# Four elementwise products and sums moved from GpSimd to VectorE in a hybrid retention and gated DeltaNet layer

## The chip, the cores and the metric

The kernel runs on one core of a Trainium2 chip. The metric is the device time of one execution in microseconds (us). Five engines of the core work side by side, each on its own list of instructions: TensorE (PE, with its weight loads shown as PEld), VectorE (DVE), ScalarE (ACT), GpSimd (POOL) and SyncE (SP), which here issues most transfers. The profile records one execution, with the clock that was granted to TensorE (1.00 is 2.4 GHz, 0.50 is 1.2 GHz).

## The reference

One decoder layer for a sequence of T = 1024 positions and a model width of 2048, all in fp32:

```python
h = x * (1 + scale) + shift                      # adaLN from c
[ret_q|ret_k|ret_v|ret_g|gdn_qkv|gdn_g|gdn_a|gdn_b] = h @ W_in
# 4 retention heads (q, k 128 wide, v 256 wide)
q, k = rotary(q), rotary(k)                      # t1*cos - t2*sin, t1*sin + t2*cos
o_ret = GroupNorm(chunkwise_retention(q, k, v)) * silu(ret_g)
# 8 gated DeltaNet heads of width 128
q, k, v = silu(causal_conv4(gdn_qkv)); q, k = l2norm(q), l2norm(k)
o_gdn = RMSNorm(chunked_delta_rule(q, k, v, decay, beta)) * silu(gdn_g)
y = concat(o_ret, o_gdn) @ W_out
out = LayerNorm(alpha * x + gate * y)
```

## The kernel before, in words

Every large matmul is done in three: an fp32 operand is split into a high part (hi) and a rest (lo), and hi·hi, hi·lo and lo·hi are summed. The weights come in units. `w_unit` loads a unit of fp32 weights by SP (`w_raw`), ACT casts it to `w_hi` (L94), and DVE subtracts to get `w_lo` (L95); each of the two has two buffers. So PE needs ACT and DVE once for every unit of weights.

The stages, in order of time: the conditioning sums, loading and transposing of x and the first projections (0 to about 197 us); `gemm_v` for the values of retention head 0 (L508, to about 245 us); eight DeltaNet heads, each with four projections `gemm_cm` (L476) and about 109 us long (to about 1107 us), with the work of retention head 0 woven into the first of them; retention heads 1 to 3 (to about 1562 us); the output projection (L1120, to about 1914 us), whose operands are split by ACT (L1065) and DVE (L1067); and a tail of DVE work.

The smaller steps are Python generators (rotary and retention, `gdn_keys`, `gdn_merge`, `gdn_scan`, `gdn_out`) that are advanced by `tick()` between the matmuls of the projections. PE's order is thus written out by hand (`tc.manual_schedule(engines={PE})`); the order on the other engines is chosen by a scheduler when the kernel is built, in which L94, L95 and the weight loads have high priority.

The names that matter here:
- `rotary` (L545 to L554) makes two products per half of the sequence into `thr` (L550, L551), one into `yr` (L552) and adds them (L553). Its table `rot` shares a buffer with the values `vt`, which ACT starts to fill at L1006.
- `retention_out` (L642 to L658): PE transposes into PSUM, ACT scales into `mxr` (L654), L656 multiplies with the gate `sg`, and a DMA issued from POOL's queue stores it (L435). `mxr` has one buffer for heads 0 to 2, so L654 of one block waits until the store of the block before has landed. The second gate tile shares its buffer with the DeltaNet values `vs` (L909), which therefore wait for its last reader at L656.
- `gdn_keys` and `gdn_merge` solve a triangular system: PE makes `sup` with DVE (L814), DVE solves blocks of 32 (`X`, L834 to L840), SP sends the result through DRAM to `Pm` (L843, L846), DVE transposes it (`Tm`, L858), and PE merges the blocks (L868).
- `gdn_scan` (L914 to L973) makes `et` (L924), transposes the queries (L929), scales them in place by a row of decays (L932), and then runs the state from chunk to chunk (PE L945, L951, L957; DVE L947, L962).
- `gdn_out` (L977 to L995): a reciprocal root `f` (L117 to L119), the product `og*f` (L985), transposes on PE (L991), the gate on DVE (L993), and a store (L435).

The lines around the four that the diff touches:

```python
S.copy(hi[:, :n], raw[:, :n])                                   # L94, ACT
V.tensor_tensor(out=lo[:, :n], in0=raw[:, :n], in1=hi[:, :n].bitcast(F32), op=ALU.subtract)   # L95
tag, bufs = ("gb", 2) if r == RH - 1 else ("mx", 1)              # retention_out
```

Of the kernel before, what the change touches and what calls it, by code (L numbers as in the profile page):

```python
# [11 lines left out]
ALU = mybir.AluOpType  # L12
# [46 lines left out]
def hybrid_layer_kernel(ctx: ExitStack, tc: tile.TileContext, x, c, w_ada, b_ada, w_in, gdn_conv_w,  # L59
# [3 lines left out]
    V, S, G, PE = nc.vector, nc.scalar, nc.gpsimd, nc.tensor  # L63
# [370 lines left out]
    def store(out, in_):  # L434
        nc.gpsimd.dma_start(out=out, in_=in_)  # L435

    def small_ps():
        return ps.tile([P, 512], F32, name="ps", tag="ps")
# [106 lines left out]
    def rotary(pt, rot, tag="th", bufs=2):  # L545
        y = mp.tile([P, T], F32, name="yr", tag="y", bufs=3)
        for i in range(2):
            sl = slice(i * 512, (i + 1) * 512)
            th = mp.tile([P, 512], F32, name="thr", tag=tag, bufs=bufs)
            V.tensor_tensor(out=th[0:64], in0=pt[64:128, sl], in1=rot[0:64, 1, sl], op=ALU.mult)  # L550
            V.tensor_tensor(out=th[64:128], in0=pt[0:64, sl], in1=rot[64:128, 1, sl], op=ALU.mult)  # L551
            V.tensor_tensor(out=y[:, sl], in0=pt[:, sl], in1=rot[:, 0, sl], op=ALU.mult)  # L552
            G.tensor_tensor(out=y[:, sl], in0=y[:, sl], in1=th, op=ALU.add)  # L553
        return y  # L554

    def retention(r, q, k, vt, sgs):
# [85 lines left out]
    def retention_out(r, pr, os_, sgs, es):  # L642
        po2 = small_ps()
        n = len(os_) * 256
        for i, e in enumerate(es):
            for j in range(2 * len(os_)):
                c0 = i * n + j * P
                PE.transpose(po2[:, c0:c0 + P], os_[j // 2][:, j % 2, e * P:(e + 1) * P], ident)
        tsl = slice(2 * pr * P, 2 * pr * P + n)
        for i, e in enumerate(es):  # L650
            kti = 2 * r + e
            tag, bufs = ("gb", 2) if r == RH - 1 else ("mx", 1)
            mx = mp.tile([P, n], F32, name="mxr", tag=tag, bufs=bufs)
            S.activation(out=mx, in_=po2[:, i * n:(i + 1) * n], func=AF.Identity,  # L654
                         scale=gnp[:, kti:kti + 1], bias=gnp[:, 8 + kti:9 + kti])
            G.tensor_tensor(out=mx, in0=mx, in1=sgs[e][:, tsl], op=ALU.mult)  # L656
            store(out=mixed[kti][:, tsl], in_=mx)
            yield 0  # L658

# [72 lines left out]
    B4 = [P, 4, P]  # L732

    def c4(t):
        return t.rearrange("p (c i) -> p c i", i=P)
# [178 lines left out]
    def gdn_scan(h, st, k, q, dec, Pm):  # L914
        kt_, vs, co = st["kt"], st["vs"], st["co"]
        *rows, et = gates.pop(h)
        ssq = gp.tile([P, NC], F32, name="ssq", tag="ssq")
        for hf in range(2):
            c4s = slice(4 * hf, 4 * hf + 4)
            pqk = small_ps()  # L920
            for j in range(4):
                cl = slice((4 * hf + j) * P, (4 * hf + j + 1) * P)
                PE.matmul(pqk[:, j * P:(j + 1) * P], k[:, cl], q[:, cl], start=True, stop=True)  # L923
            V.tensor_tensor(out=et[:, c4s], in0=c4(pqk), in1=et[:, c4s], op=ALU.mult)  # L924
            yield 2
            pq = small_ps()
            for j in range(4):
                ch = 4 * hf + j
                PE.transpose(pq[:, j * P:(j + 1) * P], q[:, ch * P:(ch + 1) * P], ident)  # L929
            sum_squares(pq, ssq[:, c4s])  # L930
            hs = slice(hf * 512, (hf + 1) * 512)
            G.tensor_tensor(out=q[:, hs], in0=q[:, hs], in1=rows[hf], op=ALU.mult)  # L932
            yield 2 + 6 * hf
        state = None
        for hf in range(2):
            o = mp.tile(B4, F32, name="og", tag="o", bufs=2)
            so = gp.tile([P, 4], F32, name="so", tag="so", bufs=2)
            for j in range(4):
                ch = 4 * hf + j
                cl = slice(ch * P, (ch + 1) * P)  # L940
                if state is None:
                    w = vs[:, ch]
                else:
                    pks = small_ps()
                    PE.matmul(pks[:, :P], k[:, cl], state, start=True, stop=True)  # L945
                    w = gp.tile([P, P], F32, name="w", tag="w", bufs=2)
                    V.scalar_tensor_tensor(out=w, in0=pks[:, :P], scalar=dec["neg"][:, ch, h:h + 1], in1=vs[:, ch],  # L947
                                           op0=ALU.mult, op1=ALU.add)
                    yield HOP[0]
                pu = small_ps()  # L950
                PE.matmul(pu[:, :P], Pm[:, ch], w, start=True, stop=True)  # L951
                u = gp.tile([P, P], F32, name="u", tag="u", bufs=2)
                S.activation(out=u, in_=pu[:, :P], func=AF.Copy, scale=co[:, ch:ch + 1])
                yield HOP[1]
                if ch < NC - 1:
                    pd = small_ps()
                    PE.matmul(pd[:, :P], kt_[:, ch], u, start=True, stop=True)  # L957
                    ns = mp.tile([P, P], F32, name="gs", tag="state", bufs=2)
                    if state is None:
                        V.tensor_copy(ns, pd[:, :P])  # L960
                    else:
                        V.scalar_tensor_tensor(out=ns, in0=state, scalar=dec["egl"][:, ch, h:h + 1], in1=pd[:, :P],  # L962
                                               op0=ALU.mult, op1=ALU.add)
                po = small_ps()
                if state is not None:
                    PE.matmul(po[:, :P], q[:, cl], state, start=True, stop=False)  # L966
                PE.matmul(po[:, :P], et[:, ch], u, start=(state is None), stop=True)  # L967
                state = ns
                S.copy(o[:, j], po[:, :P])
                junk = gp.tile([P, P], F32, name="junk", tag="xt")  # L970
                S.activation(out=junk, in_=po[:, :P], func=AF.Square, accum_out=so[:, j:j + 1])
                yield HOP[2]
            spawn_aux(gdn_out(h, hf, o, so, ssq, st), 1)  # L973

    HOP = (4, 4, 4)

    def gdn_out(h, hf, o, so, ssq, st):  # L977
        hs = slice(hf * 512, (hf + 1) * 512)
        c4s = slice(4 * hf, 4 * hf + 4)
        f = gp.tile([P, 4], F32, name="f", tag="f")  # L980
# [1 line left out]
        V.tensor_scalar(out=xo, in0=ssq[:, c4s], scalar1=1e-6, scalar2=1.28e-4, op0=ALU.add, op1=ALU.mult)  # L982
        V.scalar_tensor_tensor(out=xo, in0=so, scalar=1.0 / P, in1=xo, op0=ALU.mult, op1=ALU.add)
        rsqrt(gp, f, xo, 4, "o")
        G.tensor_tensor(out=o, in0=o, in1=f[:, :, None].broadcast_to(B4), op=ALU.mult)  # L985
        yield 36
        while "sg" not in st:
            yield 1
# [3 lines left out]
        mx = mp.tile([P, 512], F32, name="mxg", tag="mx")  # L992
# [9 lines left out]
    q = rotary(part_q0, rot, "gb", 2)  # L1002
# [15 lines left out]
    for h in range(GH):  # L1018
# [6 lines left out]
        q = conv_silu(gemm_cm(GQ + h * P), h)  # L1025
# [3 lines left out]
    for r in range(1, RH):  # L1029
# [7 lines left out]
        q = rotary(gemm_cm(RQ + r * P, True), rot)  # L1037
        k = rotary(gemm_cm(RK + r * P, True), rot)
        sgs = []
# [56 lines left out]
    for hf in range(2):  # L1096
# [4 lines left out]
        for cb in range(4):  # L1101
# [91 lines left out]
            if not last:  # L1193
                rows = []
                for n, kx in enumerate(korder):
# [15 lines left out]
                    if late and hf == 1:  # L1211
                        f, sl = late.pop(0)
# [52 lines left out]
```

## Time and profile before

| | |
|---|---|
| three runs | 1919.08, 1922.44 and 1927.89 us, median 1922.44 |
| profiled execution | 1927.46 us, its span 1925.7 us |
| mean granted clock of TensorE | 0.99 |
| PE busy | 97% of the span |
| DVE, ACT, POOL busy | 58%, 28%, 6% |

The profile is of one execution, and it is near the longest of the three runs. Matmuls are pipelined, so a row's duration overlaps the next row's; the starts tell the pace. The number in square brackets in a row of a timeline is how long the engine had been idle before it, and what it waited for.

### The profile page before, as it was taken

Reading aid. Unit: us, or ns where it says so; the run is one execution under the profiler, and the core shown is the slowest. Engines: PE = TensorE matmul, PEld = TensorE weight load, DVE = VectorE, ACT = ScalarE, POOL = GpSimd, SP = SyncE. Lnnn points to the kernel's source line nnn. Section 1 sums busy time; section 2 is a strip of 40 time slices with the busy share of each in tenths; the row PEclk is TensorE's granted clock in tenths of the full one; section 3 lists DMA queues with packets and bytes.
Section 4 is the critical chain, followed back from the end, with each engine's and each line's share of the span. In section 5 each row is a group of like instructions: output and inputs, shape, how many; then the busy total and the mean of one; then the engine's idle time right before and its main releaser. Section 6 shows DMA issues by size and latency. Waiting matters only on the chain.

```text
span 1925.7 us, 27778 instructions
## 1 busy us (share of the span) xinstructions
PE 1867.2 (97%) x10336; PEld 1582.6 (82%) x10336; DVE 1109.6 (58%) x2801; ACT 544.5 (28%) x1227; POOL 114.7 (6%) x133
## 2 busy tenths in 40 slices
PE   4999899999999999999999999999999999999997
PEld 3788878888888888888888898898898887888886
DVE  5776666574756657474655643544542544458566
ACT  2543232332323231322322121211211232235321
POOL 0000111000000000000000000100010010000000
PEclk9999999998999999999999999999999999999999
DMA  9994222221222222122212233144141157346622
GB/s 287 324 301 135 74 64 71 46 69 48 64 57 60 50 54 69 45 69 51 64 50 61 53 99 109 45 143 137 39 137 50 34 191 268 105 152 223 215 77 88
DMA packets 242474, 205.87 MB, mean 107 GB/s; under 512 B 44361, under 2 KB 200602, under 8 KB 242082
## 3 DMA queue, kind: packets, MB, share of 16 engines
q1 hardware_dynamic: 239714, 195.70, 34.3%
q0 software_dynamic: 2624, 8.39, 1.2%
q8 instruction: 81, 1.33, 0.3%
q14 instruction: 55, 0.45, 0.1%
HBM read 185.12 MB, written 18.92 MB: 106 GB/s over the span
## 4 chain that ended last, share of the span: by engine, by line
PE 79%; DVE 3%; DMA 1%; issue 0%; ACT 0%; POOL 0%; SPq 0%; POOLq 0%; DVEq 0%; ACTq 0%
PE pg L476 45%; PE po L1120 16%; PE pg L508 7%; DVE yc L666 1%; PE ps L923 1%; PE ps L951 1%; DMA raw<-mixed 1%; PE ps L967 1%; PE ps L957 1%; PE ps L811 1%; PE ps L945 1%; PE ps L966 1%; PE po L1128 1%; PE ps L603 1%; PE ps L896 0%; PE ps L889 0%
## 5 line engine op out<-in xcount | busy, mean ns | idle before, releaser
L476 PE MATMUL pg<-h_hi,w_lo 128*128 128x512 f32 x1376 | 448.0, 400 | 0.0
L476 PE MATMUL pg<-h_hi,w_hi 128*128 128x512 f32 x1376 | 446.9, 399 | 0.0
L476 PE MATMUL pg<-h_lo,w_hi 128*128 128x512 f32 x1376 | 445.0, 400 | 0.0
L1120 PE MATMUL po<-wr,ms 128*128 128x512 f32 x1380 | 314.6, 389 | 1.8 <-ACT wr L1065 1.5
L94 ACT CAST w_hi<-w_raw 128x512 fp32r<-128x512 f32 (+1 forms) x203 | 126.0, 621 | 637.2 <-PE pg L476 493.9
L1120 PEld LDWEIGHTS po<-wr,ms 128*128 128x128 f32 x1380 | 258.8, 188 | 56.3 <-ACT wr L1065 1.9
L476 PEld LDWEIGHTS pg<-h_hi,w_hi 128*128 128x128 f32 x1376 | 255.6, 189 | 49.5 <-ACT w_hi L94 1.7
L476 PEld LDWEIGHTS pg<-h_hi,w_lo 128*128 128x128 f32 x1376 | 255.7, 189 | 48.1 <-issue 0.2
L476 PEld LDWEIGHTS pg<-h_lo,w_hi 128*128 128x128 f32 x1376 | 255.3, 189 | 47.2
L95 DVE TENSOR_TENSOR w_lo<-w_raw,w_hi 128x512 fp32r<-128x512 f32 (+1 forms) x203 | 146.6, 722 | 243.7 <-ACT w_hi L94 198.4
L508 PE MATMUL pg<-w_lo,h_hi 128*128 128x256 f32 (+1 forms) x448 | 128.5, 287 | 3.4 <-DVE w_lo L95 3.4
L1067 DVE TENSOR_TENSOR wr<-raw,wr 128x512 fp32r<-128x512 f32 x116 | 80.6, 702 | 88.7 <-ACT wr L1065 84.5
L508 PE MATMUL pg<-w_hi,h_hi 128*128 128x256 f32 (+1 forms) x448 | 128.9, 288 | 1.4 <-DVE part L324 1.4
L508 PE MATMUL pg<-w_hi,h_lo 128*128 128x256 f32 (+1 forms) x448 | 128.6, 287 | 0.0
L1065 ACT CAST wr<-raw 128x512 fp32r<-128x512 f32 x116 | 71.0, 621 | 130.9 <-PE po L1120 123.2
L666 DVE SCALAR_TENSOR_TENSOR yc<-pg,cw,yc 128x1023 f32<-128x1023 f32 (+2 forms) x69 | 88.3, 1280 | 4.3 <-ACT yc L663 3.0
L508 PEld LDWEIGHTS pg<-w_lo,h_hi 128*128 128x128 f32 x448 | 86.1, 192 | 4.0 <-DVE w_lo L95 3.8
L508 PEld LDWEIGHTS pg<-w_hi,h_hi 128*128 128x128 f32 x448 | 86.1, 192 | 3.7 <-ACT w_hi L94 1.7
L508 PEld LDWEIGHTS pg<-w_hi,h_lo 128*128 128x128 f32 x448 | 86.0, 192 | 0.0
L456 DVE SCALAR_TENSOR_TENSOR gacc<-graw,cs,gacc 128x512 f32<-128x512 f32 x60 | 48.6, 810 | 50.2 <-DMA graw<-in_w_ada_dram 49.8
L208 DVE SCALAR_TENSOR_TENSOR acc<-wa,cs,acc 128x512 f32<-128x512 f32 x104 | 73.3, 746 | 6.4 <-DMA wa<-in_w_ada_dram 6.2
L307 PE MATMUL pg<-h_hi,w_hi 128*128 128x512 f32 x160 | 55.3, 428 | 8.5 <-ACT h_hi L242 8.5
(249 smaller groups left out, 2265.5 us busy)
## 6 DMA issues: line engine op xcount, KB each, us to landing
w_raw<-in_w_in_dram SPq DMA_DIRECT2D x204, 256.0 KB
wa<-in_w_ada_dram SPq DMA_DIRECT2D x128, 256.0 KB
raw<-in_w_out_dram SPq DMA_DIRECT2D x128, 256.0 KB
graw<-in_w_ada_dram SPq DMA_DIRECT2D x64, 256.0 KB
xs<-in_x_dram SPq DMA_DIRECT2D x16, 512.0 KB
raw<-mixed SPq DMA_DIRECT2D x32, 256.0 KB
z<-in_x_dram SPq DMA_DIRECT2D x32, 256.0 KB
out_dram<-z SPq DMA_DIRECT2D x32, 256.0 KB
```

Source lines behind the costliest of these rows:

```text
L94: S.copy(hi[:, :n], raw[:, :n])
L95: V.tensor_tensor(out=lo[:, :n], in0=raw[:, :n], in1=hi[:, :n].bitcast(F32), op=ALU.subtract)
L208: V.scalar_tensor_tensor(out=a, in0=wr, scalar=cs[:, r:r + 1], in1=zero.broadcast_to([P, 4 * P]) if r < 2 else a, op0=ALU.mult, op1=ALU.add)
L307: PE.matmul(ps0[t][:, i * 512:(i + 1) * 512], w[:, t * P:(t + 1) * P], hh[:, i * 512:(i + 1) * 512], start=(first and w is hi and hh is hH ...
L456: V.scalar_tensor_tensor(out=a, in0=raw[:, :512], scalar=cs[:, r:r + 1], in1=a, op0=ALU.mult, op1=ALU.add)
L476: PE.matmul(pt[:, i * 512:(i + 1) * 512], w[:, kk], hh[:, i * 512:(i + 1) * 512], start=(kt == 0 and w is hi and hh is hH[kt]), stop=(kt = ...
L508: PE.matmul(dsts[tt - tts[0]], hh[:, tsl], w[:, kk], start=(kt == 0 and first_in_bank and hh is hH[kt] and w is hi), stop=(kt == KT - 1 an ...
L603: PE.matmul(po[:, :DV], sc[:, ch], vt[:, ch], start=(ch == 0), stop=True)
L666: V.scalar_tensor_tensor(out=y[:, s:], in0=pt[:, :T - s], scalar=cw[:, j * 24 + ti:j * 24 + ti + 1], in1=y[:, s:], op0=ALU.mult, op1=ALU.add)
L1065: S.copy(t[:, :512], raw)
L1067: V.tensor_tensor(out=t[:, 512:], in0=raw, in1=t[:, :512].bitcast(F32), op=ALU.subtract)
L1120: PE.matmul(pts[tt], m[:, a + tt * P:a + (tt + 1) * P], w, start=(n == 0 and a == 0 and w is wh), stop=(n == KT - 1 and a == 512))
```

## The change

Four instructions are issued by VectorE instead of GpSimd, with the same operands and operation. They are in four functions, and stand for 68 instructions in a run: L553 16, L656 20 (eight of 128x256 for retention head 0, twelve of 128x512), L932 16 and L985 16. GpSimd keeps its memsets (L826, L827, L853, L1017) and the issue of the stores (L435).

```diff
@@ rotary
             V.tensor_tensor(out=y[:, sl], in0=pt[:, sl], in1=rot[:, 0, sl], op=ALU.mult)
-            G.tensor_tensor(out=y[:, sl], in0=y[:, sl], in1=th, op=ALU.add)
+            V.tensor_tensor(out=y[:, sl], in0=y[:, sl], in1=th, op=ALU.add)
@@ retention_out
-            G.tensor_tensor(out=mx, in0=mx, in1=sgs[e][:, tsl], op=ALU.mult)
+            V.tensor_tensor(out=mx, in0=mx, in1=sgs[e][:, tsl], op=ALU.mult)
             store(out=mixed[kti][:, tsl], in_=mx)
@@ gdn_scan
             hs = slice(hf * 512, (hf + 1) * 512)
-            G.tensor_tensor(out=q[:, hs], in0=q[:, hs], in1=rows[hf], op=ALU.mult)
+            V.tensor_tensor(out=q[:, hs], in0=q[:, hs], in1=rows[hf], op=ALU.mult)
@@ gdn_out
         rsqrt(gp, f, xo, 4, "o")
-        G.tensor_tensor(out=o, in0=o, in1=f[:, :, None].broadcast_to(B4), op=ALU.mult)
+        V.tensor_tensor(out=o, in0=o, in1=f[:, :, None].broadcast_to(B4), op=ALU.mult)
```

PE's order is the same in both kernels, row for row. DVE's and ACT's change, since the scheduler places the new instructions and moves others. The first place is DVE's list in the first rotary, during `gemm_v` of head 0 (`part_106`, `part_108` and `part_109` are the projections of k, q and a gate):

```order
 L550 TENSOR_TENSOR thr<-part_108,rot 64x512
 L551 TENSOR_TENSOR thr<-part_108,rot 64x512
 L552 TENSOR_TENSOR yr<-part_108,rot 128x512
+L95 TENSOR_TENSOR w_lo<-w_raw,w_hi 128x544
+L553 TENSOR_TENSOR yr<-yr,thr 128x512
 L550 TENSOR_TENSOR thr<-part_106,rot 64x512
-L95 TENSOR_TENSOR w_lo<-w_raw,w_hi 128x544
 L551 TENSOR_TENSOR thr<-part_106,rot 64x512
 L552 TENSOR_TENSOR yr<-part_106,rot 128x512
 L550 TENSOR_TENSOR thr<-part_106,rot 64x512
+L553 TENSOR_TENSOR yr<-yr,thr 128x512
 L551 TENSOR_TENSOR thr<-part_106,rot 64x512
```

The split of a weight unit moves from behind the first product of the second tensor to ahead of it, and the sums stand between the products. Further on the next split moves in the same way, from behind the gate's pair L534 to ahead of the last L552.

The second place is DVE's list where the last four blocks of retention head 0 go out, about 297 to 312 us, beside the start of the first DeltaNet head:

```order
-L95 TENSOR_TENSOR w_lo<-w_raw,w_hi 128x512
-L909 TENSOR_TENSOR vs<-ps,sk 128x512 x2
+L814 SCALAR_TENSOR_TENSOR sup<-ps,nco,et 128x128 x3
+L95 TENSOR_TENSOR w_lo<-w_raw,w_hi 128x512
+L814 SCALAR_TENSOR_TENSOR sup<-ps,nco,et 128x128 x5
+L656 TENSOR_TENSOR mxr<-mxr,sg 128x256 x2
+L95 TENSOR_TENSOR w_lo<-w_raw,w_hi 128x512
+L656 TENSOR_TENSOR mxr<-mxr,sg 128x256
 L95 TENSOR_TENSOR w_lo<-w_raw,w_hi 128x512
 L666 SCALAR_TENSOR_TENSOR yc<-pg,cw,yc 128x1023
+L656 TENSOR_TENSOR mxr<-mxr,sg 128x256
 L666 SCALAR_TENSOR_TENSOR yc<-pg,cw,yc 128x1022
```

Four gate products now stand between the splits of weights and the first steps of a convolution (L666), and the pair L909 has moved behind them, in between the steps of the block solve.

The third place is DVE's list at the end of the second half of a DeltaNet head (here head 2):

```order
 L118 TENSOR_TENSOR rs_o<-rs_o,f 128x4
 L119 SCALAR_TENSOR_TENSOR f<-rs_o,f 128x4
+L985 TENSOR_TENSOR og<-og,f 128x512
 L794 TENSOR_TENSOR ktok<-ps,ktl 128x512
 L95 TENSOR_TENSOR w_lo<-w_raw,w_hi 128x512
```

The product follows right behind the step that makes `f`.

## Rows read from the trace of the kernel before

**Rows 1.** The page, busy time, share of the span and instructions of each engine.

```profile
PE 1867.2 (97%) x10336; PEld 1582.6 (82%) x10336; DVE 1109.6 (58%) x2801; ACT 544.5 (28%) x1227; POOL 114.7 (6%) x133
```

**Rows 2.** Waits of PE: line, releaser, us in total, times, longest.

```profile
PE pg L508 <- DVE w_lo L95: 3.4, 2, 2.7
PE ps L991 <- POOL og L985: 2.9, 3, 1.2
PE po L1120 <- ACT wr L1065: 1.5, 1, 1.5
...
PE ps L908 <- DVE sup L814: 1.2, 1, 1.2
PE ps L868 <- DVE Tm L858: 0.8, 1, 0.8
...
PE ps L945 <- DVE gs L962: 0.4, 1, 0.4
```

**Rows 3.** Groups of POOL by line: busy us, mean ns, idle before.

```profile
L553 POOL TENSOR_TENSOR yr<-yr,thr 128x512 f32<-128x512 f32 x16 | 22.6, 1414 | 432.4 <-DVE yr L552 432.4
L656 POOL TENSOR_TENSOR mxr<-mxr,sg 128x512 f32<-128x512 f32 (+1 forms) x20 | 22.1, 1103 | 203.5 <-ACT mxr L654 181.7 <-DMA w_raw<-in_w_in_dram 21.7
L932 POOL TENSOR_TENSOR yc<-yc,gr 128x512 f32<-128x512 f32 x16 | 21.2, 1323 | 125.8 <-PE ps L929 125.8
L985 POOL TENSOR_TENSOR og<-og,f 128x512 f32<-128x512 f32 x16 | 17.1, 1068 | 200.0 <-DVE f L119 137.4 <-ACT gr L758 29.6 <-ACT og L969 22.4
```

**Rows 4.** Groups of DVE by line, same columns.

```profile
L1067 DVE TENSOR_TENSOR wr<-raw,wr 128x512 fp32r<-128x512 f32 x116 | 80.6, 702 | 88.7 <-ACT wr L1065 84.5 <-DMA lnb_b<-in_ln_b_dram 2.0 <-DMA raw<-in_w_out_dram 2.0
...
L598 DVE SCALAR_TENSOR_TENSOR rs<-rs,ps 128x256 f32<-128x256 f32 x24 | 9.9, 414 | 1.8 <-PE ps L593 1.7
```

**Rows 5.** Timeline of PE, 211 to 226 us: start, us, work, idle before.

```profile
213.73 0.39 PE L508 MATMUL pg<-w_lo,h_hi 128*128 128x272 f32 x1 [0.68 <-DVE w_lo L95]
...
221.24 0.59 PE L508 MATMUL pg<-w_lo,h_hi 128*128 128x272 f32 x1 [2.71 <-DVE w_lo L95]
```

**Rows 6.** Windows of 4 us: busy and count by engine, PE clock, DMA share, GB/s.

```profile
220.00:224.00 4.00, 2.76 (x12) 2.76 (x13) 1.99 (x5) 0.00 (x0) 1.93 (x4) 0.59 0.33 77
224.00:228.00 4.00, 4.00 (x33) 4.00 (x33) 0.09 (x1) 0.65 (x1) 0.00 (x0) 0.99 0.21 62
```

**Rows 7.** Timeline of DVE, 205 to 232 us.

```profile
206.70 2.39 DVE L672 SCALAR_TENSOR_TENSOR yc<-th,yc 128x512 f32<-128x512 f32 x2
...
212.04 1.64 DVE L95 TENSOR_TENSOR w_lo<-w_raw,w_hi 128x544 fp32r<-128x544 f32 x1
...
215.85 1.69 DVE L551 TENSOR_TENSOR thr<-part,rot 64x512 f32<-64x512 f32 x1
...
218.19 2.36 DVE L534 SCALAR_TENSOR_TENSOR sg<-th,part 128x512 f32<-128x512 f32 x2
220.47 0.71 DVE L95 TENSOR_TENSOR w_lo<-w_raw,w_hi 128x544 fp32r<-128x544 f32 x1
```

**Rows 8.** Timeline of POOL, 709 to 713 us.

```profile
710.84 1.03 POOL L985 TENSOR_TENSOR og<-og,f 128x512 f32<-128x512 f32 x1 [9.73 <-ACT gr L758]
```

**Rows 9.** Timeline of DVE, 1562 to 1570 us.

```profile
1567.84 2.29 DVE L1067 TENSOR_TENSOR wr<-raw,wr 128x512 fp32r<-128x512 f32 x1
```

**Rows 10.** Timeline of DVE, 332 to 343 us.

```profile
338.83 1.46 DVE L858 STREAM_TRANSPOSE Tm<-Pm 32x32 f32<-32x32 f32 x13
```

**Rows 11.** Timeline of PE, 340 to 353 us and 440 to 459 us.

```profile
342.05 0.89 PE L868 MATMUL ps<-Tm,sup 32*32 32x32 f32 x32
...
443.98 0.89 PE L868 MATMUL ps<-Tm,sup 32*32 32x32 f32 x24 [0.82 <-DVE Tm L858]
```

**Rows 12.** Window 444 to 462 us, columns as in rows 6.

```profile
444.00:462.00 18.00, 18.00 (x145) 14.62 (x146) 6.51 (x23) 0.84 (x5) 1.30 (x2) 0.62 0.06 15
```

**Rows 13.** Timeline of ACT, 293 to 313 us.

```profile
308.61 0.56 ACT L654 ACTIVATE mxr<-ps,gnp 128x256 f32<-128x256 f32 x1 [6.02 <-DMA mixed<-mxr]
```

**Rows 14.** Timeline of DVE, 293 to 313 us.

```profile
310.02 1.29 DVE L909 TENSOR_TENSOR vs<-ps,sk 128x512 f32<-128x512 f32 x2 [7.60 <-POOL mxr L656]
```

## The prediction

> **What bounds the kernel now.** I read the page's busy shares first. TensorE works 97% of the span, VectorE 58%, GpSimd 6% [rows 1]. The span is therefore TensorE's list, and a change to the other engines can only move the places where TensorE waits, or where its clock is low. GpSimd's 115 us cost nothing by themselves. Next come TensorE's waits [rows 2]: apart from the start, which the change doesn't reach, the reader sees a handful of waits of about a microsecond, and two of them name what the change touches, 3.4 us for the split of a weight unit in the first rotary and 2.9 us for the output scaling L985. So the gain from waits is a few microseconds at most. The granted clock comes third: after the longer wait TensorE runs a few microseconds at a low clock [rows 6], so a wait there costs more than its length. Last, the timelines of the engines around each place give what VectorE would do instead.
>
> **What an instruction costs on either engine.** The four groups take 22.6 + 22.1 + 21.2 + 17.1 = 83 us on GpSimd [rows 3]. VectorE has no such instruction in this kernel, but L1067 has the same form, two fp32 inputs in SBUF of 128x512, at 0.70 us, and L598 stands near the 128x256 form at 0.41 us [rows 4]. So VectorE gets 60 × 0.70 + 8 × 0.41 = 45 us more, and would be busy about (1110 + 45)/1926 = 60%, which doesn't make it the bound. VectorE gets something back too. While GpSimd adds, a VectorE instruction with two SBUF inputs takes much longer: the split L95 takes 1.64 us where it takes 0.71 a little later, L551 takes 1.69, against the 0.70 of that form, and the pairs L672 and L534 2.39 and 2.36, against about 1.4 for two such [rows 4, 7]. Each is longer by about 1 us, which is about the time of the add still to run. With the adds on VectorE this lengthening goes, and 0.70 us for the add itself comes: a little gain for VectorE where the two engines met, a loss of 0.70 where they did not.
>
> **First rotary, 196 to 224 us: −4.7 us.** VectorE is without a pause here. Four adds on GpSimd lengthen four pieces by 0.93 + 0.99 + 1.0 + 1.0 = 3.9 us [rows 7]; on VectorE four adds cost 2.8. More than that counts the order: the split of the next unit moves ahead of the first product of the second tensor, and the following one ahead of the last product and the gate. From the starts in [rows 7] with 0.7 us per instruction, the first add, three products and the split after the pair L672 (which ends at 206.70 + 1.4 = 208.1) end at about 211.6 instead of 213.68, and TensorE asks for that split at 213.05 (213.73 less 0.68). Four products and two adds later, the second split ends at about 217.2 instead of 221.18; TensorE asks at 218.53 (221.24 less 2.71), earlier by the 0.7 it no longer waited, thus at 217.85. So both waits, 0.68 + 2.71 = 3.4 us [rows 5], go. After the longer one the clock is 0.59, and 12 matmuls take 2.76 us, 0.23 each, where the next window does 33 in 4.00, 0.12 each [rows 6]: 12 × 0.11 = 1.3 us more. Sum −4.7. The second split has only 0.7 us to spare. ACT's cast for it stands behind the fill of `vt`, which waits for the last reader of `rot`; if the cast is late by 1 us, 0.3 to 1 us of the 4.7 stays. Ends: −5 and −2.
>
> **Output scaling: −1.4 us.** In three heads TensorE's transposes L991 wait for L985, 2.9 us together [rows 2]. GpSimd begins about 0.16 us behind `f` and takes 1.03 [rows 8]; VectorE goes on with its next instruction, 0.70 [rows 4]. That is 0.47 each. What stands before is as it was, so 1.5 us of wait remain. In the first halves L985 now stands ahead of the state update L962 in VectorE's list, 0.70 us. For that update TensorE's L945 waits once, 0.4 us [rows 2], so in the other heads there is something to spare; I take 0, and at worst the whole 0.70 for eight heads, +5.6.
>
> **Into the output projection: −0.5 us.** Around 1566 us the last gates on GpSimd lengthen L1067, from 0.70 to 2.29 in one case [rows 9], 1.6 us; two gates of 0.70 come on VectorE, 1.4. TensorE's wait there, 1.5 us for ACT's L1065 [rows 2], hangs on a transfer of the stored `mixed`. The store goes out up to a microsecond earlier. Ends −1.5 and +0.5.
>
> **Retention head 0: +0.7 us.** Eight products of 0.41 us come onto a VectorE that is busy there, 3.3 us, against perhaps 0.8 of lengthening that goes. TensorE waits for `sup` already, 1.2 us [rows 2]. The first four products stand ahead of that, but `sup` also hangs on ACT and DRAM. I take +0.7, between 0 (they fall into VectorE's pauses) and +2.5 (all of it shows). The second four stand ahead of weight splits and of the block solve; what that can do is the third rival. I estimate that the block solve ends 1.4 us later. The transposes `Tm` end at 338.83 + 1.46 = 340.29, and TensorE wants them at 342.05 [rows 10, 11]: 1.76 to spare, so nothing is lost, with 0.4 left.
>
> **Everything else: 0.** The 16 query scalings come into VectorE's pauses, and the first product of queries and state is some matmuls away in TensorE's list. The rotary sums and gates of the later retention heads run beside projections, with VectorE idle 42% of the span [rows 1]; head 3's gates are in the term on the output projection. If that cover failed throughout, 16 + 12 + 8 = 36 instructions of 0.70 would give +25. But the page's pauses are many times longer than these, and the few waits for VectorE in [rows 2] are none of them for these lines, so I take 0 and give the upper end little weight.
>
> **Sum.** −4.7 − 1.4 − 0.5 + 0.7 = −5.9 us. The profiled execution took 1927.46, so 1921.6 on its scale. It stands 5.0 above the median of the runs shown, 1922.44; on the median's scale the forecast is 1916.5. About 0.5%, 9.6 us, is what a measurement of this kernel can tell from no change, so the likeliest outcome is inside that, on the fast side. Its own range, with the ends above and 3 us of spread between runs: 1911 to 1922.
>
> **Rivals.**
>
> *The second head's stall goes too.* In head 1 TensorE waits 0.82 us for `Tm` [rows 11], and from 444 to 462 us it is granted 0.62 of its clock while it is busy all of the time [rows 12]: 18 × 0.38 = 6.8 us. For it: VectorE is relieved of lengthening in the block solve before it, and 0.82 us is little. Against: the chain goes through DRAM, and the scaling L932 and the products of head 0 add to VectorE. Then −5.9 − 0.8 − 6.8 = −13.5, 1909.
>
> *The first head's merge falls into the same stall.* The 1.76 us to spare at 342 us [rows 10, 11] are used up by late splits and late stores. For it: head 1 shows what less slack brings. Against: my estimate leaves 0.4. Price 0.5 + 6.8 = 7.3 us: 1916.5 + 7.3 = 1924. If a pause of 0.8 us doesn't lower the clock, only the 0.5 remains and this rival can't be told from the forecast. The Trainium skill says in "TensorE: Matmul & The Clock Gate", Part 1, that idleness throttles the array's clock and sustained work releases it; by that rule the 2.71 us ahead of the window at 0.59 fits, and a stall of 0.5 us alone should leave the clock at full, so that this rival would come out at 1917. The trace speaks against the rule here, with 0.62 granted after 0.82 us of idling, if it is the wait that did it; small matmuls on a corner of the array stand around it.
>
> *A gate product holds VectorE up (slower).* In VectorE's new list four gates L656 stand ahead of weight splits and of L666. Each waits for ACT's L654, and that waits until the store of the block before has landed, 6.02 us of idling on ACT in one case [rows 13]. VectorE has stood 7.60 us behind such a gate already, at L909 with the next split behind it [rows 14]. Before, only that pair stood behind the gate; now everything on VectorE does. From the point where a store lands more than about 4 us late, a split comes later than TensorE's two buffers cover, and TensorE waits some 4 us, followed by a slow clock as in [rows 12], 6.8, while the gains stay: 1922.4 − 5.9 + 10.8 = 1927, and if it happens for two of the four, 1933 or more. For it: the order. Against: in the old times the gates are ready about when the splits are, within 1 us. The slower side is reached only here.
>
> *The gain moves on.* What TensorE doesn't wait for in the first rotary it waits for at the next unit, since the loads and casts paced by TensorE catch up with it. Then 1922. For it: DMA has a share of 0.33 at that place [rows 6], and ACT and SP are issued in order. Against: the next units are there after 224 us without a wait.
>
> **Chances.** Forecast 0.47, second head too 0.14, first head's merge 0.16, VectorE held up 0.09, gain moves on 0.14. The range reaches from the second rival's lower side to the held-up case: 1907 to 1928, with about one in ten left out on either side. Faster by over 0.5% (below 1912.8): most of the second head's case and a fifth of the forecast's, 0.24. Slower by over 0.5% (above 1932): half of the held-up case and something unforeseen, 0.07. The rest, 0.69, is within.
>
> **What the new profile would show.** Right: no wait of L508 for L95 between 205 and 225 us and a granted clock of 1.0 from 220 to 224; three waits L991 for VectorE's L985 of about 0.5 us; no 1.6 us L95 beside a GpSimd add; VectorE near 60%, GpSimd near 2%. Wrong: a wait of L476 for `w_lo` between 297 and 312 us, a VectorE row there whose idle time ends with ACT's L654, a wait of L868 near 342 us with a clock near 0.6 behind it (it rests on an estimate of 1.4 us), or new waits of L945 for L962.

## The result, and the profile after

The changed kernel took 1911.13 us (median of 7 runs, 1910.37 to 1917.55), the kernel before 1925.22 us (7 runs, 1919.08 to 1928.38): ratio 0.9942, 95% interval 0.9924 to 0.996, so 0.4% to 0.8% faster. The profiled execution took 1911.13 us with a span of 1909.4, against 1925.7 before: 16.3 us less. The forecast was 1916.5 and a gain of 5.9. One execution of an experiment below, the profiled one of the gates alone, was granted 0.66 of the clock throughout and took 2670.68 us; no ratio and no reading rests on it.

The page of the changed kernel, busy time, answers to [rows 1]. VectorE has 68 instructions more. They take 45 us, as the prediction has it, but VectorE's busy time grew by 20 us only, because its other instructions take 25 us less; GpSimd went from 115 to 30 us.

```profile
PE 1858.8 (97%) x10336; PEld 1577.2 (83%) x10336; DVE 1129.3 (59%) x2869; ACT 544.6 (29%) x1227; POOL 30.4 (2%) x65
```

The groups of VectorE by line (busy us, mean ns, idle before) give the four edits' prices, 0.69 us for a 128x512:

```profile
L656 DVE TENSOR_TENSOR mxr<-mxr,sg 128x512 f32<-128x512 f32 (+1 forms) x20 | 11.5, 580 | 17.7 <-ACT mxr L654 17.7
L985 DVE TENSOR_TENSOR og<-og,f 128x512 f32<-128x512 f32 x16 | 11.1, 692 | 0.5
L932 DVE TENSOR_TENSOR yc<-yc,gr 128x512 f32<-128x512 f32 x16 | 11.0, 690 | 2.0 <-PE ps L929 1.6
L553 DVE TENSOR_TENSOR yr<-yr,thr 128x512 f32<-128x512 f32 x16 | 11.0, 686 | 0.2
```

The waits of TensorE answer to [rows 2]. The two waits for the splits in the first rotary, 3.4 us, are gone; the 0.2 us that L508 still waits for a split stand at 1273.73 us, in retention head 2. The waits for L985 fell from 2.9 to 1.6 us; those of L908, L945 and L1120 are no longer there; the one for `Tm` stayed.

```profile
PE ps L602 <- DVE rs L596: 1.9, 1, 1.9
PE ps L991 <- DVE og L985: 1.6, 3, 0.7
...
PE ps L868 <- DVE Tm L858: 0.9, 1, 0.9
...
PE pg L508 <- DVE w_lo L95: 0.2, 1, 0.2
```

TensorE's list is the same in both kernels, 10,336 matmuls, so the nth of one trace can be set against the nth of the other. How much earlier or later it starts is the lag, and where the lag changes, time was gained or lost. Worked out that way (us; the last two columns come from the runs below):

| stretch, time before | forecast | whole change | edit alone | whole change without it |
|---|---|---|---|---|
| first rotary, 197 to 230 | −4.7 | −5.1 | −5.1 (L553), and −1.3 in the runs of L985 and of L656 alone | |
| three waits L991 | −1.4 | −1.3 | −1.4 (L985) | |
| state update L945, 584 | 0 | −0.5 | −0.5 (L985) | |
| retention head 0, 250 to 310 | +0.7 | −1.1 | −1.3 (L656) | wait L908 back, +1.6 |
| into the output projection | −0.5 | −2.4 | −1.7 (L656) | +1.4 |
| second head, 425 to 480 | 0 | −5.7 | +0.2 to +0.4 for three edits, −5.6 for L656 | +5.7 |
| rest | 0 | −0.2 | | |

The rest holds −0.6 in the first 150 us, which no edit reaches and where the traces below differ from the kernel before by −1.8 to +1.4, and +0.5 at 1288 us, at the split of retention head 2.

The row of the second head isn't a wait: it is the granted clock. The window that answers to [rows 12] starts right behind the same wait for `Tm`, and has the clock at full where the kernel before had 0.62:

```profile
437.30 0.90 PE L868 MATMUL ps<-Tm,sup 32*32 32x32 f32 x24 [0.93 <-DVE Tm L858]
```

```profile
437.00:455.00 18.00, 17.70 (x175) 14.77 (x176) 9.85 (x31) 4.46 (x21) 0.52 (x1) 1.00 0.15 36
```

### The profile page after: what moved, and what is told of

Its sections match the earlier page's. It is cut to its first block, busy times and chain, and to the rows that moved or that the text cites. A ratio compares the mean times of both kernels' runs of the same rounds, so it can differ in the third digit from the quotient of the medians.

```text
span 1909.4 us, 27676 instructions
## 1 busy us (share of the span) xinstructions
PE 1858.8 (97%) x10336; PEld 1577.2 (83%) x10336; DVE 1129.3 (59%) x2869; ACT 544.6 (29%) x1227; POOL 30.4 (2%) x65
## 4 chain that ended last, share of the span: by engine, by line
PE 91%; DVE 4%; DMA 3%; ACT 1%; SPq 1%; issue 0%; DVEq 0%; ACTq 0%
PE pg L476 47%; PE po L1120 18%; PE pg L508 7%; PE pg L307 5%; DMA wa<-in_w_ada_dram 1%; DVE yc L666 1%; PE ps L951 1%; DMA graw<-in_w_ada_dram 1%; PE ps L923 1%; PE ps L811 1%; PE ps L967 1%; PE ps L603 1%; PE ps L957 1%; PE ps L508 1%; PE ps L945 1%; PE ps L602 1%
## 5 line engine op out<-in xcount | busy, mean ns | idle before, releaser
L1120 PE MATMUL po<-wr,ms 128*128 128x512 f32 x1380 | 314.0, 389 | 0.0
L1120 PEld LDWEIGHTS po<-wr,ms 128*128 128x128 f32 x1380 | 258.9, 188 | 53.7
L95 DVE TENSOR_TENSOR w_lo<-w_raw,w_hi 128x512 fp32r<-128x512 f32 (+1 forms) x203 | 140.3, 691 | 221.3 <-ACT w_hi L94 176.0
L508 PE MATMUL pg<-w_hi,h_hi 128*128 128x256 f32 (+1 forms) x448 | 128.3, 286 | 1.4 <-DVE part L324 1.4
L508 PE MATMUL pg<-w_hi,h_lo 128*128 128x256 f32 (+1 forms) x448 | 128.1, 286 | 0.0
L508 PE MATMUL pg<-w_lo,h_hi 128*128 128x256 f32 (+1 forms) x448 | 127.8, 285 | 0.2 <-DVE w_lo L95 0.2
L666 DVE SCALAR_TENSOR_TENSOR yc<-pg,cw,yc 128x1023 f32<-128x1023 f32 (+2 forms) x69 | 88.3, 1279 | 4.9 <-ACT yc L663 3.6
L508 PEld LDWEIGHTS pg<-w_hi,h_hi 128*128 128x128 f32 x448 | 85.5, 191 | 3.5 <-ACT w_hi L94 1.7
L508 PEld LDWEIGHTS pg<-w_lo,h_hi 128*128 128x128 f32 x448 | 85.5, 191 | 0.6 <-DVE w_lo L95 0.4
L508 PEld LDWEIGHTS pg<-w_hi,h_lo 128*128 128x128 f32 x448 | 85.5, 191 | 0.0
L456 DVE SCALAR_TENSOR_TENSOR gacc<-graw,cs,gacc 128x512 f32<-128x512 f32 x60 | 45.1, 751 | 54.7 <-DMA graw<-in_w_ada_dram 54.1
```

The costliest lines, as they stand in the source:

```text
L456: V.scalar_tensor_tensor(out=a, in0=raw[:, :512], scalar=cs[:, r:r + 1], in1=a, op0=ALU.mult, op1=ALU.add)
L508: PE.matmul(dsts[tt - tts[0]], hh[:, tsl], w[:, kk], start=(kt == 0 and first_in_bank and hh is hH[kt] and w is hi), stop=(kt == KT - 1 an ...
L666: V.scalar_tensor_tensor(out=y[:, s:], in0=pt[:, :T - s], scalar=cw[:, j * 24 + ti:j * 24 + ti + 1], in1=y[:, s:], op0=ALU.mult, op1=ALU.add)
L1120: PE.matmul(pts[tt], m[:, a + tt * P:a + (tt + 1) * P], w, start=(n == 0 and a == 0 and w is wh), stop=(n == KT - 1 and a == 512))
```

## Experiments

Each run was profiled once, and timed with the kernel before on the same chip where a ratio is given.

**One edit at a time.** Each is the kernel before with one of the four lines of the diff.

> Of the four edits only the rotary sums (L553) go to VectorE. By my theory (each edit acts at its own place, set against TensorE's identical list of matmuls): TensorE's two waits for the split in the first rotary and the slow clock behind them go, 5.1 us between 205 and 225 us, and nothing elsewhere, so the waits L991 (2.9 us), L908 (1.2 to 1.6) and the one into the output projection (1.5 to 2.4) stay as before; time about 5 us under before at the same clock in the second head. Rival (the edits help each other, since what VectorE loses to GpSimd at one place it gives back only when all have left): under 3 us here. Rival (the gain moves on): the 5 us come back as waits in the next units, 0 to 1 us left.

Measured: 1921.29 us (12 runs) against 1924.95 (35 runs), ratio 0.998, interval 0.9966 to 0.9993. In TensorE's list −5.14 us between 197 and 230 us, and behind the start at no other place a gain; the waits L991, L908 and those into the output projection are there. At the last of these the list lost 2.3 us, mostly since this execution was granted half the clock for 3.4 us there. Both rivals fall, and the first theory has the size. But 1.3 of the 5.1 us are the clock behind the longer wait, and that comes by the run: the runs of L985 and of L656 alone below keep the wait of 2.71 us, have the full clock behind it, where the kernel before had 0.59 [rows 6], and so gain the same 1.3 us without this edit. This is the run of L985 alone:

```profile
222.62 0.39 PE L508 MATMUL pg<-w_lo,h_hi 128*128 128x272 f32 x1 [2.71 <-DVE w_lo L95]
```

```profile
222.00:226.00 4.00, 3.38 (x27) 3.39 (x28) 1.37 (x4) 0.00 (x0) 1.36 (x3) 1.00 0.45 115
```

The clock fell there in two of the four traces with this wait (before, and L932 alone) and in none of the nine without it. What the edit gives in every run is the rest, 3.9 us.

> Only the retention gates (L656) go to VectorE. It is the one edit that changes the lists of ScalarE and SyncE. My theory: about 1.1 us less around 255 to 300 us (the wait L908 for sup goes, a wait L602 for rs comes), and 2.4 us less at about 1590 us, into the output projection, so 3.5 us; the rotary waits (3.7 us) and the L991 waits (2.9) stay. Rival: the 2.4 us at the output projection come from the other edits' relief of VectorE, or from the state of the transfers, then under 1.5 us in all. Rival from the prediction (gate products hold VectorE up): waits for w_lo at 290 to 312 us, and slower than before by 2 us or more.

Measured: 1921.39 us (median of 12 runs, the one at 0.66 among them), ratio 0.9984, interval 0.9969 to 1.0. The waits come from a second profiled execution of the same edit:

> Only the retention gates (L656) on VectorE, a second execution with a profile, because the profiled one before was at a granted clock of 0.66 throughout. My theory: no wait L908 for sup (1.2 to 1.6 us in the kernel before and with the gates on GpSimd), a wait L602 for rs of up to 0.5 us more, and the wait at the entry into the output projection below 0.5 us where the kernel before has 2.4. Rival: that wait varies by itself and is there (1 us or more); then the gates are worth about 1 us.

Measured: 1920.39 us (one run); no wait L908, the waits L602 2.3 us together against before's 2.2, and of the wait into the output projection 0.3 us are left. These are waits of TensorE in it; the two of the first rotary, those for L985 and the one of L945 are as before, and L508 has a third wait for a split, 1.1 us:

```profile
PE pg L508 <- DVE w_lo L95: 4.5, 3, 2.7
PE ps L991 <- POOL og L985: 2.9, 3, 1.2
PE ps L602 <- DVE rs L596: 1.7, 1, 1.7
...
PE ps L945 <- DVE gs L962: 0.4, 1, 0.4
PE po L1120 <- DVE wr L1067: 0.3, 1, 0.3
```

In TensorE's list −1.3 us in retention head 0 and −1.7 into the output projection; −1.3 in the first rotary and −5.6 in the second head, both by the clock; and +1.4 at 1288 us of before's time, in retention head 2. That is the third wait. The split stands there behind a sum L456, for which VectorE waited 2.42 us for a transfer:

```profile
1280.87 0.75 DVE L456 SCALAR_TENSOR_TENSOR gacc<-graw,cs,gacc 128x512 f32<-128x512 f32 x1 [2.42 <-DMA graw<-in_w_ada_dram]
1281.54 0.69 DVE L95 TENSOR_TENSOR w_lo<-w_raw,w_hi 128x512 fp32r<-128x512 f32 x1
```

```profile
1282.28 0.39 PE L508 MATMUL pg<-w_lo,h_hi 128*128 128x256 f32 x1 [1.10 <-DVE w_lo L95]
```

A wait at this place, 0.2 to 1.1 us, is in six of the eight traces with the gates on VectorE and in none of the five with the gates on GpSimd. How the gates bring it about is open; the prediction put the later retention heads at 0.

The timeline of VectorE in this run shows where the wait L908 went: the factors for `sup` (L803 to L806) are made 1.5 us earlier.

```profile
294.26 0.17 DVE L806 TENSOR_SCALAR nco<-co 128x8 f32<-128x8 f32 x1
294.55 0.87 DVE L814 SCALAR_TENSOR_TENSOR sup<-ps,nco,et 128x128 f32<-128x128 f32 x3
```

In the kernel before the same step stands at

```profile
295.79 0.17 DVE L806 TENSOR_SCALAR nco<-co 128x8 f32<-128x8 f32 x1
296.08 0.61 DVE L814 SCALAR_TENSOR_TENSOR sup<-ps,nco,et 128x128 f32<-128x128 f32 x2
```

The list has put the two rounds of the reciprocal root for `rk` ahead of the products L629, where they stood behind before; that is the scheduler's new order, and not in the price of an instruction. Part of the 1.5 us is something else: in the kernel before two steps of VectorE ahead of L806 were lengthened beside gates on GpSimd, L629 from 0.73 (the pair in the whole change) to 1.15 and L119 from 0.16 to 0.60,

```profile
286.63 1.15 DVE L629 TENSOR_SCALAR o<-o,mv,rstd 128x256 f32<-128x256 f32 x2
...
293.95 0.60 DVE L119 SCALAR_TENSOR_TENSOR rk<-rs_k,rk 128x8 f32<-128x8 f32 x1
```

```profile
286.06 1.24 POOL L656 TENSOR_TENSOR mxr<-mxr,sg 128x256 f32<-128x256 f32 x1 [2.27 <-ACT mxr L654]
...
293.75 0.77 POOL L656 TENSOR_TENSOR mxr<-mxr,sg 128x256 f32<-128x256 f32 x1 [5.58 <-ACT mxr L654]
```

0.9 us together. No run changes the order and leaves the gates on GpSimd, so the two shares aren't told apart.

> Only the output scaling (L985) goes to VectorE. My theory: 0.47 us each at the three waits L991, 1.3 to 1.4 us in all, and 0.5 us at about 584 us, where GpSimd's product lay on a split ahead of the state update (L945 waits for L962); 1.9 us in all, which a single time can hardly tell from nothing but TensorE's list can. Rival: on VectorE it delays the state update, then waits L945 of 0.3 us or more in several heads and no gain.

Measured: 1921.85 us, ratio 0.9988, interval 0.9972 to 1.0004. In TensorE's list −0.51, −0.40 and −0.49 at the three waits, and −0.47 at 584 us, with no new wait of L945: 1.9 us. The time can't show it, the list does. The only other gains behind the start are the clock's 1.3 us in the first rotary and 0.4 into the output projection.

> Only the query scaling (L932) goes to VectorE. My theory: no effect on TensorE's list beyond 0.3 us anywhere (VectorE's pauses take 11 us more, and the products that GpSimd lengthened were not waited for). Rival: the scaling lengthened the block solve of the heads, so that the wait L868 in the second head (0.82 us) and the slow clock behind it go, 6 to 7 us, in all runs. Rival: it stands ahead of the state copy L960, and L945 waits 0.3 us or more in several heads, slower by 2 us.

Measured: 1924.86 us, ratio 1.0001, interval 0.9986 to 1.0016. Behind the start nothing over 0.5 us in TensorE's list but −0.9 into the output projection, long after the last query is scaled. The query scalings are free, as the first theory had it; the wait for `Tm` and the slow clock behind it stayed.

**The change without the gates.** The changed kernel with L656 on GpSimd.

```diff
-            V.tensor_tensor(out=mx, in0=mx, in1=sgs[e][:, tsl], op=ALU.mult)
+            G.tensor_tensor(out=mx, in0=mx, in1=sgs[e][:, tsl], op=ALU.mult)
```

> The whole change without the retention gates, which stay on GpSimd. My theory: 5.1 us at the first rotary (3.8 of waits, the rest clock) and 1.9 us at L991 and L945, nothing else; against the whole change TensorE's list then shows +1.1 us around 255 to 300 us (the wait L908 for sup is back, the wait L602 for rs smaller) and about +2.4 us at the entry into the output projection (before's 2.4 us of waits back). So about 3.5 us slower than the whole change at the same clock. Rival: the entry into the output projection gains without the gates too, since the transfers there vary by themselves (the single edits had waits there of 1.4 to 3 us): then the gates are worth about 1 us.

Measured: 1918.73 us, ratio 0.9971, interval 0.9952 to 0.999. Against the whole change TensorE's list shows +1.6 us where the wait L908 is back and +1.4 into the output projection, and +5.7 in the second head, where this execution's clock fell:

```profile
PE ps L908 <- DVE sup L814: 1.3, 1, 1.3
...
PE po L1120 <- ACT wr L1065: 0.3, 1, 0.3
PE po L1120 <- DVE wr L1067: 0.3, 1, 0.3
```

The first theory holds for L908. For the output projection the rival has a share: that wait varies by itself. In the traces with the gates on GpSimd it is 1.8, 2.2, 1.4, 0.9 and 0.6 us long (before, and the runs of L553, L985 and L932 alone, and this one), with the gates on VectorE 0, 0.3, 0.3, 0, 0, 0, 1.1 and 0. So the gates are worth about 1.4 − 0.2 = 1.2 us there, and the 2.4 of the profiled pair has luck in it.

**GpSimd sums put back beside the new list.** The changed kernel, with a sum on GpSimd beside each of the four of the first rotary.

```diff
+    again = lambda v, on: on and G.tensor_tensor(out=mp.tile([P, 512], F32, name='dm', tag='mx'), in0=v, in1=v, op=ALU.add)
...
-            V.tensor_tensor(out=y[:, sl], in0=y[:, sl], in1=th, op=ALU.add)
+            V.tensor_tensor(out=y[:, sl], in0=y[:, sl], in1=th, op=ALU.add); again(y[:, sl], dummy)
```

> The whole change, with VectorE's sums in the first rotary, and beside each of the four a GpSimd sum of the same size (128x512, from the finished yr, into a tile that nothing reads). All other lists are the same as in the whole change. Theory A (what hurts is that VectorE's instructions with two SBUF inputs stand still while GpSimd adds): three or four VectorE instructions there last about 1 us longer again, the second split of weights comes about 2 to 3 us later and TensorE waits 1 to 3 us for it; 1 to 4 us slower there. Theory B (what hurt was the place of the splits behind GpSimd's latency, and the order the scheduler chose): the splits come as in the whole change, no wait, 0 us.

Measured: +1.9 us in TensorE's list between 197 and 230 us, with one wait of 1.67. First the changed kernel's VectorE there, which answers to [rows 7]:

```profile
210.06 0.72 DVE L95 TENSOR_TENSOR w_lo<-w_raw,w_hi 128x544 fp32r<-128x544 f32 x1
...
212.09 0.69 DVE L551 TENSOR_TENSOR thr<-part,rot 64x512 f32<-64x512 f32 x1
...
215.73 0.73 DVE L95 TENSOR_TENSOR w_lo<-w_raw,w_hi 128x544 fp32r<-128x544 f32 x1
```

then the same instructions in this experiment, with the order of VectorE's list unchanged,

```profile
209.85 0.72 DVE L95 TENSOR_TENSOR w_lo<-w_raw,w_hi 128x544 fp32r<-128x544 f32 x1
...
211.90 1.44 DVE L551 TENSOR_TENSOR thr<-part,rot 64x512 f32<-64x512 f32 x1
...
216.30 1.39 DVE L95 TENSOR_TENSOR w_lo<-w_raw,w_hi 128x544 fp32r<-128x544 f32 x1
```

and its GpSimd:

```profile
211.31 1.47 POOL L544 TENSOR_TENSOR dm<-yr 128x512 f32<-128x512 f32 x1 [2.66 <-DVE yr L553]
215.63 1.47 POOL L544 TENSOR_TENSOR dm<-yr 128x512 f32<-128x512 f32 x1 [2.85 <-DVE yr L553]
```

L551 and L95 begin during a GpSimd sum, and end 0.6 us after it ends (211.31 + 1.47 = 212.78 against 213.34; 217.10 against 217.69): they do most of their own 0.7 us once the sum is over. Each is 0.7 us longer, not 1, and so is the L551 ahead of them, beside the first sum. Theory A holds for 1.9 us of the 5.1, and theory B, which had 0 here, falls. The clock did not fall at this place here; it has 1.3 us of the 5.1. What is left, about 2, would be the moved splits: that is a remainder and not shown by a run, since the GpSimd sums of this run don't stand where those of the kernel before did. The Trainium skill says it in "SBUF — State Buffer", "SBUF: two separate sides": a VectorE operation with two inputs in SBUF and a GpSimd operation that reads SBUF take a shared port in turn, and the later one stands still until the other has ended. These rows agree.

**The clock in the second head.** In both kernels the times come in groups that go with the mean granted clock of the execution. The runs at 0.995 have medians of 1919.3 (10 runs of the kernel before, of 68) and 1911.1 (9 of the changed one, of 17); the changed kernel's runs at 0.991 are at 1916.25 to 1918.34. In the profiled runs the fall in the second head, a stretch at half the clock, is most of the difference. It was in the profiled run of before and not in that of after, behind nearly the same wait.

> The whole change again, as the control for the other three on the same chip: about 1911 us, with some runs of about 1917 at a lower granted clock; if the slower ones come from the second head's half clock alone, they are 5.5 to 6.5 us above the others. Theory (half clock as often as in the kernel before): more than half of the runs near 1917; rival (2 of 7, as measured): about a third.

Measured: 1914.21 us (10 runs), ratio 0.995, interval 0.9931 to 0.9968: four runs at 0.995, 1911.03 to 1912.47, four at 0.991, 1916.25 to 1918.34, two between. This time the profiled run has a fall in the second head, half as long as before's. So the fall is not a thing that the change takes away. Over the 17 runs of the changed kernel six are at 0.991 and two between, a share between a third and a half, which doesn't decide between the two theories on it.

> The whole change, and in the second DeltaNet head the merge L868 starts five matmuls later in TensorE's list, so that its wait of 0.93 us for Tm goes. Theory A (the wait is what lets the clock fall): the half clock from 446 to 460 us is seen in no run, the granted clock is 0.995 in all and the times are about 1910, without the ones of 1917. Theory B (the clock falls because of the small matmuls on a corner of the array around it, by the phase of the chip's own clock control): some of the runs still have 0.991 and 1916 to 1918. In both the 0.9 us go, unless a later step of the head is then late.

```diff
-        yield MERGE_WAIT
+        yield MERGE_WAIT + late
...
-        spawn(gdn_merge(st, Pm))
+        spawn(gdn_merge(st, Pm, 5 if h == 1 else 0))
```

Measured: 1917.0 us, ratio 0.9961, interval 0.9946 to 0.9977. The edit didn't do its job: a split got in between the transposes, the wait stayed at 0.80 us, and the clock fell behind it. This doesn't tell the theories apart.

> The whole change, and in the second DeltaNet head the merge L868 starts fourteen matmuls later (3.2 us) in TensorE's list. With five, the wait for Tm stayed, 0.80 us, because a split of weights came in between the transposes Tm, and the clock fell as before. With fourteen, Tm (ready at 437.9 to 438.4) should be ready before TensorE asks (about 439.1), so no wait L868 in the second head. Theory A (a wait ahead of the small matmuls is what lets the clock fall): no fall in the second head, granted clock 0.995 in nearly all runs, times about 1910 to 1912. Theory B (the small matmuls alone do it at that place): falls in about half of the runs, 1916 to 1918. If another head gets the wait instead, theory A has the fall there.

Measured (14 in place of 5): 1912.75 us (8 runs), ratio 0.9952, interval 0.9933 to 0.9971. The wait is gone, `Tm` comes 0.3 us ahead of need, and the profiled run has no fall:

```profile
436.79 1.27 DVE L858 STREAM_TRANSPOSE Tm<-Pm 32x32 f32<-32x32 f32 x11
```

```profile
438.38 0.89 PE L868 MATMUL ps<-Tm,sup 32*32 32x32 f32 x32
```

But two of its eight runs are at 0.991 and 0.992, 1917.86 and 1917.96 us. These two have no profile, so where their clock fell isn't known. Low clocks became no rarer than the samples can tell (the whole change had 0.991 in 6 of 17 runs); theory A isn't shown.

> The whole change, and in the second DeltaNet head the four groups of small matmuls of the merge (32x32 and 64x64) stand ten to eleven matmuls of the projection apart instead of four or five. Theory A (the clock falls where small matmuls follow each other closely): no fall at about 440 us in any run, granted clock 0.995 in all, times at 1910 to 1912. Theory B (it falls at that place for another reason): falls in about half of the runs, 1916 to 1918, as with the whole change.

The edit adds 6 to the four pauses (4, 5, 4, 5) of the second head's merge.

Measured: 1919.65 us, ratio 0.9975, interval 0.9963 to 0.9988, slower than the whole change. Spreading the small matmuls didn't keep the clock up: most runs are at 0.991. But it moved later work so that the third head now waits for `Tm`, and there the profiled run's long fall is, in a head that has neither wait nor fall in any other trace; a short one, 3.4 us, stands in the second head behind a wait of 1.06 us. Timeline of TensorE and window:

```profile
546.51 0.89 PE L868 MATMUL ps<-Tm,sup 32*32 32x32 f32 x24 [0.90 <-DVE Tm L858]
```

```profile
546.00:564.00 18.00, 17.49 (x141) 13.82 (x142) 8.13 (x29) 1.02 (x4) 0.52 (x1) 0.62 0.10 26
```

So in all nine traces with a fall in a head, it comes behind a wait L868 of 0.8 to 1.1 us; but in three traces a wait of 0.92 to 0.97 us has no fall behind it, and in the first rotary the clock fell behind the 2.71 us in two traces and stayed at full in two. By the rule that the prediction took from the Trainium skill, "TensorE: Matmul & The Clock Gate", Part 1, idleness throttles the array. These traces agree in so far as every fall in a head stands behind a wait. What decides in the single run is open.

> The whole change, and the transposes L991 of each half head stand four matmuls of the projection later in TensorE's list. The three waits for L985 that are left (1.6 us) should go, 0.9 us of matmul time being enough to cover 0.55; time about 1.5 us under the whole change at the same clock. Rival: the wait is paced from elsewhere (ScalarE's copies of og, the transposes of the next head), and comes back there; 0 us. The falls of the clock in the second head should come as often as before, and set most of the spread of the times.

The edit makes `yield 36` into `yield 40` in `gdn_out`.

Measured: 1911.35 us (6 runs), ratio 0.9933, interval 0.9917 to 0.995. The three waits L991 went, 2.2 us in TensorE's list, but the wait into the output projection was there (1.1 us, and 1.6 of lag), and +0.4 came at 580 us. At 0.995 its runs are at 1911.42 and 1911.66, as the whole change's. It isn't faster beyond what can be measured, so no version beats the changed kernel here.

## Why the prediction was right, and where it was off

**The bound.** Right: TensorE's list set the time in both, and the 20 us more of VectorE's busy time cost nothing by themselves; only the waits and the clock moved.

**First rotary.** Right in mechanism for the waits, and right in size with luck: −5.1 against −4.7. The splits came at 210.06 and 215.73 and ended at 210.78 and 216.46, in a run that was 0.6 us ahead since the start (forecast 211.6 and 217.2; the prediction counts four products between them, the list has five, and the 217.2 allows for five). TensorE waits for no split there instead of 3.4 us, and the window at 220 us has a clock of 1.00. The waits were worth 3.9 us, the prediction had 3.4. Its other term, 1.3 us of clock, has the right size for the profiled pair, but it is there in only two of the four traces with this wait. The run with GpSimd sums put back gives the standstill 1.9 us; the remainder, about 2, is left for the new order.

**Output scaling.** Right for the waits: −1.3 against −1.4, 0.7 left of 1.2 in the longest (from its rows it comes to 0.49 each and not 0.47). The state update, put at 0 to +5.6, gained 0.5: the GpSimd product had lengthened the split ahead of it to 1.42 us (582.68 us, beside the product at 582.51), and the prediction looked for such lengthening at the rotary and the output projection only.

**Into the output projection.** Right in sign, and mis-sized: −0.5 against −2.4 in the pair, about −1.2 over the traces; the rest of the pair's 2.4 is luck. The lengthening [rows 9] did go, and the gates now stand between splits of 0.69 us:

```profile
1553.16 0.68 DVE L1067 TENSOR_TENSOR wr<-raw,wr 128x512 fp32r<-128x512 f32 x1
1553.76 0.68 DVE L656 TENSOR_TENSOR mxr<-mxr,sg 128x512 f32<-128x512 f32 x1
```

**Retention head 0.** Wrong in sign: the step that failed is "+0.7, between 0 and +2.5". It measured −1.1. The prediction set eight products against "perhaps 0.8" of lengthening, about what the trace has, and left out that the new order would help to put the factors of `sup` 1.5 us earlier; the lower end should have been below nothing. The order of the two kernels showed the moved L117 to L119, and I had read it only for the gates. The estimate that the block solve would end 1.4 us later failed too: `Tm` ended at 330.81 + 2.64 = 333.45, 1.8 us ahead of need at 335.26, as before.

```profile
330.81 2.64 DVE L858 STREAM_TRANSPOSE Tm<-Pm 32x32 f32<-32x32 f32 x24 [2.02 <-DMA Pm<-s]
```

```profile
335.26 0.89 PE L868 MATMUL ps<-Tm,sup 32*32 32x32 f32 x32
```

**The gate product that holds VectorE up.** It didn't decide. VectorE does stand behind ScalarE's L654, as that rival said:

```profile
295.18 0.43 DVE L656 TENSOR_TENSOR mxr<-mxr,sg 128x256 f32<-128x256 f32 x1 [3.17 <-ACT mxr L654]
295.69 0.69 DVE L95 TENSOR_TENSOR w_lo<-w_raw,w_hi 128x512 fp32r<-128x512 f32 x1
...
306.23 0.43 DVE L656 TENSOR_TENSOR mxr<-mxr,sg 128x256 f32<-128x256 f32 x1 [3.00 <-ACT mxr L654]
```

but no store landed late enough: TensorE has no wait for a split there. The 0.2 us for a split in retention head 2 stand behind L456 and not behind a gate; the prediction put those heads at 0.

**The second head.** The rival "the second head's stall goes too" had the right price, 6.8 against 5.7 us, and the wrong reason: the wait it hung on stayed, 0.82 before and 0.93 after, and only the clock differed, by the run. The prediction took the profiled run's clock for a property of the kernel, here and in the 1.3 us of the first rotary.

**The sum.** Without the second head the pair differs by 16.3 − 5.7 = 10.6 us; less the clock in the rotary, which not every run has, and the luck at the output projection, 1.3 and 1.2, that is 8.1. The runs at 0.995 differ by 1919.3 − 1911.1 = 8.2. Both agree with what the single edits give: 3.9 in the rotary, 1.9 for L985, 1.3 and about 1.2 for L656, together 8.3, of which the split in retention head 2 takes back 0.5 (1.4 in the run of L656 alone). So 7.8 to 8.3 us is the change's worth, against the 5.9 forecast. The medians differ by 14.1 us, and in the second measurement by 10 (1924.26 against 1914.21); what goes beyond the 8 is taken to be how often the clock fell in the runs, which is argued from the groups and not shown run by run. So the measured 1911.13 lies at the lower edge of the forecast's own range and nearer the 1909 of the second head's rival, but not for that rival's reason. (The upper end of that range, 1922, follows from the ends without the 3 us of spread; with them it would be 1925.)

## What to carry to other kernels

Where one engine's list is written out and the same in both kernels, set its instructions against each other one by one: gains of 0.5 us at their places are sure there, while the run's time can't show them. An elementwise step on GpSimd is not free because GpSimd is idle; ask which VectorE instruction with two SBUF inputs it stands beside, and who waits for that. And before a stretch of low clock is priced into a forecast, see in several runs whether it belongs to the kernel or to the run.

## What was unexpected of the hardware

A 128x512 sum or product takes 1.07 to 1.41 us on GpSimd [rows 3] and 0.69 on VectorE, and moving 83 us of such work added only 20 us to VectorE's busy time. The clock of TensorE fell to half for 3.4 to 13.7 us behind waits of 0.8 to 1.1 us, while the engine was busy for 18.00 of 18.00 us in one window [rows 12], in the second head of nine of the thirteen profiled executions and in the third head of one of these; the same kernel had it in one execution and not in another.
